# Loading the second half of the first tile by four transfers over 112, 16, 13 and 3 partitions

## The chip, the cores and the metric

The kernel runs on one core of one Trainium2 chip. The metric is the device time of one execution in microseconds (us); the time before is 469.24 us, the median of three executions (469.23 to 469.35). The profile and the trace are those of one further execution of 469.19 us, of which the profiler shows a span of 467.9 us.

In this kernel three of the core's engines do something: the scalar engine (ACT) computes the GELU, the vector engine (DVE) multiplies, and the sync engine (SP) does nothing but issue loads and the last stores. The bytes themselves are carried between HBM and SBUF by 16 DMA engines, which all transfers share. "DMA engine" always means one of these sixteen below.

## The reference

```python
def setup_inputs():
    batch, seq, dim = (32, 512, 2048)
    return {'x': np.random.randn(batch, seq, dim).astype(np.float32)}

def reference(x):
    half_dim = x.shape[-1] // 2
    x1, x2 = x[..., :half_dim], x[..., half_dim:]
    gelu_x1 = 0.5 * x1 * (1 + erf(x1 / np.sqrt(2)))
    return (gelu_x1 * x2).astype(np.float32)
```

Of each row of 2048 float32 numbers, the GELU of the first 1024 is multiplied by the other 1024. There are 16,384 rows: 134.2 MB are read and 67.1 MB written.

## The kernel before

The rows are taken in 16 tiles. A tile has 128 partitions with 8 rows in each, so that a partition's share of a load is one run of 64 KB in HBM and in SBUF, and of a store one run of 32 KB. Two input buffers and two output buffers are used in turn.

```python
R = 8
x_t = x_flat.rearrange("(n p r) d -> n p r d", p=P, r=R)      # P = 128, 16 tiles
o_t = out_flat.rearrange("(n p r) d -> n p r d", p=P, r=R)
x_bufs = [nc.alloc_sbuf_tensor(f"x{k}_tile", [P, R, dim], x.dtype) for k in range(2)]
o_bufs = [nc.alloc_sbuf_tensor(f"o{k}_tile", [P, R, half], out.dtype) for k in range(2)]
first = [nc.alloc_semaphore(f"first{j}") for j in range(2)]
ready = [nc.alloc_semaphore(f"ready{k}") for k in range(2)]
# ... more semaphores, and n[...], which counts what each was increased by ...

def load(i, rows, sem):
    ins = nc.sync.dma_start(out=x_bufs[i % 2][:, rows, :], in_=x_t[i][:, rows, :])   # L47
    counted(ins, sem, 16)
    return ins

def store(queue, i, rows, sem):
    queue.wait_ge(mul_done, n[mul_done.name])
    counted(queue.dma_start(out=o_t[i][:, rows, :],                                  # L54
                            in_=o_bufs[i % 2][:, rows, :]), sem, 16)

# the first tile in two halves, then the second tile whole
for ins in (
    load(0, slice(0, 4), first[0]),
    load(0, slice(4, 8), first[1]),
    load(1, slice(0, 8), ready[1]),
):
    ...

for i in range(n_tiles):
    k = i % 2
    last = i == n_tiles - 1
    pieces = i == 0 or last
    steps = ((0, 2), (2, 4), (4, 8)) if pieces else ((0, 5), (5, 8))
    for lo, hi in steps:
        rows = slice(lo, hi)
        if i == 0 and lo % 4 == 0:
            nc.scalar.wait_ge(first[lo // 4], 16)
        elif lo == 0:
            nc.scalar.wait_ge(ready[k], n[ready[k].name])
        # ACT:  o = gelu(x1)          (L81)
        # DVE:  o = o * x2            (L89), waits for the GELU
        if pieces and hi % 4 == 0:
            # store this half of the tile: from the scalar queue, the last tile's from SP
            ...
    if not pieces:
        # store the tile: from the scalar queue, that of the last but one from SP
        ...
    if i + 2 < n_tiles:
        nc.sync.wait_ge(mul_done, n[mul_done.name])
        load(i + 2, slice(0, R), ready[k])
```

The load of tile i + 2 is issued when tile i has been multiplied, as both use the same input buffer.

## Time and profile before

| what | before |
|---|---|
| time, median of 3 | 469.24 us (469.23 to 469.35) |
| span in the profile | 467.9 us |
| busy time of DVE | 140.5 us (30%) |
| busy time of ACT | 115.5 us (25%) |
| moved from and to HBM | 134.22 MB read, 67.11 MB written, 430 GB/s over the span |
| first half of the first tile landed, GELU begins | 12.76 us |
| second half landed, GELU begins | 22.46 us |
| second tile landed, GELU begins | 47.20 us |
| end of the last multiplication | 460.2 us |

How it is read: a share of the span beside an engine is its busy time. The landing times are the starts of the first GELU instructions after a wait for a load. The trace also holds a record of each DMA packet (start, duration, size, queue; not which of the sixteen engines carried it): a packet here is one partition's run, of 32 KB in the two loads of the first tile, 64 KB in the other loads, 32 KB in a store of a whole tile and 16 KB in a store of half a tile.

### The profile page before, as it was taken

Reading aid. Unit: us, or ns where it says so; the run is one execution under the profiler, and the core shown is the slowest. Engines: PE = TensorE matmul, PEld = TensorE weight load, DVE = VectorE, ACT = ScalarE, POOL = GpSimd, SP = SyncE. Lnnn points to the kernel's source line nnn. Section 1 sums busy time; section 2 is a strip of 40 time slices with the busy share of each in tenths; the row PEclk is TensorE's granted clock in tenths of the full one; section 3 lists DMA queues with packets and bytes.
Section 4 is the critical chain, followed back from the end, with each engine's and each line's share of the span. In section 5 each row is a group of like instructions: output and inputs, shape, how many; then the busy total and the mean of one; then the engine's idle time right before and its main releaser. Section 6 shows DMA issues by size and latency. Waiting matters only on the chain.

```text
span 467.9 us, 152 instructions
## 1 busy us (share of the span) xinstructions
DVE 140.5 (30%) x34; ACT 115.5 (25%) x35; POOL 0.2 (0%) x4
## 2 busy tenths in 40 slices
DVE  0330514207052060511606116060150702507043
ACT  1320606042060410604106050050500506014060
POOL 0000000000000000000000000000000000000000
DMA  8999999999999999999999999999999999999998
GB/s 359 448 448 443 403 405 492 409 403 448 459 437 403 434 417 493 403 403 448 476 420 403 445 406 493 403 406 445 487 409 403 445 451 448 403 434 417 493 389 373
DMA packets 5041, 201.34 MB, mean 430 GB/s; under 512 B 560, under 2 KB 560, under 8 KB 560
## 3 DMA queue, kind: packets, MB, share of 16 engines
q1 hardware_dynamic: 2880, 142.61, 70.6%
q10 hardware_dynamic: 2160, 58.72, 29.1%
q14 instruction: 1, 0.01, 0.0%
HBM read 134.22 MB, written 67.11 MB: 430 GB/s over the span
## 4 chain that ended last, share of the span: by engine, by line
DMA 76%; DVE 14%; ACT 8%; ACTq 0%; SPq 0%; issue 0%
DMA out_dram<-o_tile 66%; DVE o_tile L89 14%; DMA x_tile<-in_x_dram 10%; ACT o_tile L81 8%; ACTq L112 0%; SPq L47 0%
## 5 line engine op out<-in xcount | busy, mean ns | idle before, releaser
L89 DVE TENSOR_TENSOR o_tile<-o_tile,x_tile 128x5120 f32<-128x5120 f32 (+3 forms) x34 | 140.5, 4171 | 319.7 <-ACT o_tile L81 319.7
L81 ACT ACTIVATE o_tile<-x_tile 128x5120 f32<-128x5120 f32 (+3 forms) x34 | 114.3, 3407 | 337.4 <-DMA out_dram<-o_tile 301.6
L81 ACT ACT_TABLE_LOAD x1 | 1.3, 1283 | 2.9 <-PEq L67 2.9
L135 POOL MEMSET const-bfloat16-1.0<- 128x1 bf16 x1 | 0.1, 101 | 0.0
L135 POOL MEMSET const-uint8-127<- 128x1 uint8 x1 | 0.1, 101 | 0.0
L135 POOL MEMSET const-float32-0.0<- 128x1 f32 x1 | 0.1, 98 | 0.2 <-issue 0.2
L135 POOL MEMSET const-float32-1.0<- 128x1 f32 x1 | 0.1, 98 | 0.0
## 6 DMA issues: line engine op xcount, KB each, us to landing
out_dram<-o_tile ACTq DMA_DIRECT2D x13, 4096.0 KB, 44.7
x_tile<-in_x_dram SPq DMA_DIRECT2D x2, 4096.0 KB, 16.6
out_dram<-o_tile ACTq DMA_DIRECT2D x2, 2048.0 KB, 34.5
out_dram<-o_tile SPq DMA_DIRECT2D x1, 4096.0 KB, 25.2
out_dram<-o_tile SPq DMA_DIRECT2D x2, 2048.0 KB, 7.8
x_tile<-in_x_dram SPq DMA_DIRECT2D x15, 44.2
```

Of the source, the lines that this page charges most:

```text
L81: nc.scalar.activation(out=o_bufs[k][:, rows, :], in_=x_bufs[k][:, rows, :half], func=GELU),
L89: nc.vector.tensor_mul(out=o_bufs[k][:, rows, :], in0=o_bufs[k][:, rows, :], in1=x_bufs[k][:, rows, half:],),
L135: nc = _bacc.Bacc("TRN2", target_bir_lowering=False, num_devices=1)
```

## The change

The load of rows 4 to 7 of the first tile, which was one transfer over 128 partitions, becomes four transfers on the same queue: rows 4 to 7 of partitions 0 to 111; rows 4 to 6 of partitions 112 to 127; row 7 of partitions 112 to 124; row 7 of partitions 125 to 127. One row is 8 KB. If the first two are shared by all 16 DMA engines, the third by 13 and the fourth by 3, thirteen of the sixteen carry at least as much as before and three carry less: the engines' shares, 256 KB each before, become 264 KB for three, 256 KB for ten and 248 KB for three. It is meant to even out small differences between the moments at which the DMA engines finish. The wait for the second half is raised from 16 to the sum of the four transfers' increments, 64; nothing else differs.

```diff
-    def load(i, rows, sem):
-        ins = nc.sync.dma_start(out=x_bufs[i % 2][:, rows, :], in_=x_t[i][:, rows, :])
+    def load(i, rows, sem, parts=slice(0, P)):
+        ins = nc.sync.dma_start(out=x_bufs[i % 2][parts, rows, :], in_=x_t[i][parts, rows, :])
         counted(ins, sem, 16)
         return ins
 ...
         load(0, slice(0, 4), first[0]),
-        load(0, slice(4, 8), first[1]),
+        load(0, slice(4, 8), first[1], slice(0, 112)),
+        load(0, slice(4, 7), first[1], slice(112, 128)),
+        load(0, slice(7, 8), first[1], slice(112, 125)),
+        load(0, slice(7, 8), first[1], slice(125, 128)),
         load(1, slice(0, 8), ready[1]),
 ...
             if i == 0 and lo % 4 == 0:
-                nc.scalar.wait_ge(first[lo // 4], 16)
+                nc.scalar.wait_ge(first[lo // 4], n[first[lo // 4].name])
```

## The prediction

> **What bounds the kernel now.** I read the head of the page first: engines, the forty slices, DMA.

> ```profile
> span 467.9 us, 152 instructions
> DVE 140.5 (30%) x34; ACT 115.5 (25%) x35; POOL 0.2 (0%) x4
> ...
> DMA  8999999999999999999999999999999999999998
> ...
> q1 hardware_dynamic: 2880, 142.61, 70.6%
> q10 hardware_dynamic: 2160, 58.72, 29.1%
> q14 instruction: 1, 0.01, 0.0%
> HBM read 134.22 MB, written 67.11 MB: 430 GB/s over the span
> ```

> The compute engines are busy 30% and 25%. The DMA row has nines except in its end slices, and the two data queues together take 70.6 + 29.1 = 99.7% of all sixteen DMA engines' time. There is next to nothing left to fill: the bound is bytes per DMA engine.

> The chain that ended last says the same, step after step of it being a transfer; its beginning is what the change touches:

> ```profile
> 1.64 45.54 DMA x_tile<-in_x_dram
> 47.18 0.02 issue
> 47.20 4.48 ACT o_tile L81
> 51.68 0.02 issue
> 51.70 8.77 DVE o_tile L89 x2
> 60.48 0.02 issue
> 60.50 40.04 DMA out_dram<-o_tile
> ```

> The ACT and DVE links in it are no time without transfers. I asked for the busy time by stage, cut where the first half, second half and second tile land and where the last tile's GELU begins (columns: stretch, its length, DVE, ACT and POOL busy with counts, clock, DMA share, GB/s):

> ```profile
> 0.00:12.74 12.74, 0.00 (x0) 1.28 (x1) 0.20 (x4) 1.00 0.91 370
> 12.74:22.44 9.70, 4.49 (x2) 3.71 (x2) 0.00 (x0) 1.00 1.15 486
> 22.44:47.18 24.74, 4.42 (x1) 3.62 (x1) 0.00 (x0) 1.00 0.98 424
> 47.18:448.54 401.36, 122.65 (x28) 99.72 (x28) 0.00 (x0) 1.00 1.00 432
> ```

> In the 401 us of the middle the DMA share is 1.00 at 432 GB/s while DVE works 123 us. (The 1.15 is packets booked to one side of a cut.) Last I took the packet records themselves. They don't name the DMA engine, but each packet starts within some nanoseconds of another's end, so they can be strung into sixteen chains. The sixteen first packets start at 1.74 to 2.30 us, the sixteen last end at 466.92 to 467.43 us, and no chain has a gap of more than 3 ns. Each chain carries 12.58 MB; a 32 KB packet takes 1.21 us (27 GB/s), one of 64 KB 2.42 us. Of the sixteen ends, two are late: 467.40 (the chain with the one 8 KB instruction packet of 0.31 us, at 460.9 us) and 467.43 (the chain that started last, at 2.30 us). Then come 467.26 and 467.23, the others being at 467.15 or before.

> So whatever one DMA engine loses, anywhere, it finishes later by the same amount, and the slowest of sixteen sets the end. There is no slack to take it up, except that an engine which isn't last has up to 467.43 - 466.92 = 0.5 us.

> [...]

> **The change part by part.**

> *Shares.* 224 + 24 + 8 + 8 = 264 KB for the first three engines, 256 KB for ten, 224 + 24 = 248 KB for the last three. 8 KB is a quarter of a packet of 1.21 us, 0.30 us. If nothing else changed, the best is the case that the latest finishers get less: 467.43 would become 467.13, and the next one, 467.40, has to be among the relieved too. Then 467.26 stands (if it isn't), a gain of 0.17 us. The worst is that the chain at 467.40 is one of the three that get more: 467.70, a loss of 0.27 us. As the first three start first (1.74 to 1.75 us, if starts go by number) and the chain with the instruction packet started at 1.744 us, I lean to the loss. Either way 0.06% at most.

> *Issue.* Three more issues on SP at about 0.43 us (the longest of the loads' issue times in the trace) delay the second tile's load by 1.3 us. It was issued by 1.64 us and isn't needed until the second half has been carried, about 20 us. Nothing on the path.

> *Waits.* The wait for 64 instead of 16 adds none by itself. If the second half lands late by a few us, GELU, multiplication, the store of that half (30.57 us) and the load of the third tile shift likewise; the DMA engines still have the second tile's 8 packets of 2.42 us, 19.3 us, to carry, against 22.46 to 30.57 = 8.1 us of compute and issue, so none runs dry.

> *Ports.* This is the part that matters, [...] The 112-partition transfer: 7 packets per engine. If each takes 7 partitions in a row (that is my assumption; [...]), engines start at partitions 0, 7, 14, ... 105; [...] Engines 0 to 2 then lose 2.42 + 2.72 + 0.91 + 0.61 + 0.30 (their own 8 KB) = 6.96 us; less the up to 0.5 us by which they were early, the end moves by 6.5 to 7.0 us: 475.7 to 476.2 us.

> **The rivals.** First, [...] only the shares count, 469.07 to 469.51 us. For it: the change aims at tenths of a us, and someone who tunes on that scale will have seen how the DMA engines finish. [...] I give it 25%.

> Second, the limit holds but costs half: [...] 3 to 5 us, 472 to 474 us. Nothing in the trace speaks for or against. With the full count, 60%.

> Third, the 112 partitions are dealt one by one, engine after engine. Then at each step the sixteen engines write sixteen neighbouring partitions, [...] so up to 498 us and slower by 6%. [...] 15%.

> **Range and chances.** The middle of this mixture lies in the port case, somewhat below its full count: 474.0 us. The range takes in the first rival at its low end and the full count with some 2 us to spare: 468.9 to 478.4. The 2% lines are 459.9 and 478.6 us; faster is out of reach, since the whole idle time at the ends is about 5 us; above 478.6 lies the third rival nearly alone: 0.12.

> **What would show it.** With the ports right, the packet records of the changed kernel have packets of 24 KB at up to 3.6 us and of 8 KB at around 1.2 us instead of 0.9 and 0.3, and 32 KB packets at 1.21 and 2.42 us mixed; the second half lands at 26 to 30 us instead of 22.46; the second tile lands 4 to 7 us later than 47.18; and the sixteen chains end apart by some us instead of 0.5. With the first rival, 24 KB take 0.91 us, the landing moves by under 0.5 us and the ends stay within 0.8 us. I am wrong altogether if 24 KB packets run alone at full speed and the time still moves by more than 0.3 us, or if they are slow and the end doesn't move: then the engines had slack that I don't see.

## The result and the profile after

The changed kernel takes 477.1 us (median of five runs, 476.86 to 477.24) against 469.28 us for the kernel before in the same session (469.23 to 469.35): a ratio of 1.0165, 95% interval 1.0151 to 1.0179. That is 7.8 us slower. The prediction had 474.0 us with a range of 468.9 to 478.4, and 475.7 to 476.2 for the full sum of its port case.

The head of the page of the changed kernel, to be laid beside the lines shown of before:

```profile
span 475.9 us, 155 instructions
DVE 140.5 (30%) x34; ACT 115.5 (24%) x35; POOL 0.2 (0%) x4
...
DMA  8999999999999999999999999999999999999998
GB/s 353 286 332 430 437 443 408 427 452 441 421 438 443 408 432 457 438 410 449 446 405 435 454 441 410 454 435 424 421 443 421 441 454 430 427 419 443 441 410 362
...
q1 hardware_dynamic: 2928, 142.61, 70.8%
q10 hardware_dynamic: 2160, 58.72, 28.8%
HBM read 134.22 MB, written 67.11 MB: 423 GB/s over the span
```

Compute is the same to a tenth of a us, the bytes are the same, and the DMA engines are as busy as before: the row of nines has not changed. What has changed are two slices of the GB/s row, which in the kernel before reads:

```profile
GB/s 359 448 448 443 403 405 492 409 403 448 459 437 403 434 417 493 403 403 448 476 420 403 445 406 493 403 406 445 487 409 403 445 451 448 403 434 417 493 389 373
```

In the second and third slice (11.9 to 35.7 us) the same busy DMA engines move 286 and 332 GB/s; before it was 448 and 448. From the fourth slice on nothing is unusual. This is a loss that a busy share cannot show: a packet that takes longer (1.969 us for 32 KB where it was 1.213, as the packet records below show) keeps its engine busy longer.

The stages, cut where the halves and the second tile land and where the last tile's GELU begins (columns as in the prediction):

```profile
0.00:12.97 12.97, 0.00 (x0) 1.28 (x1) 0.20 (x4) 1.00 0.93 364
12.97:35.21 22.24, 4.49 (x2) 3.71 (x2) 0.00 (x0) 1.00 0.99 287
35.21:57.33 22.12, 4.42 (x1) 3.62 (x1) 0.00 (x0) 1.00 1.02 441
57.33:456.00 398.67, 122.64 (x28) 99.72 (x28) 0.00 (x0) 1.00 1.00 433
456.00:475.88 19.88, 8.92 (x3) 7.22 (x3) 0.00 (x0) 1.00 0.91 389
```

The last stage of the kernel before, for comparison:

```profile
448.54:467.90 19.36, 8.92 (x3) 7.21 (x3) 0.00 (x0) 1.00 0.95 407
```

From the first half's landing to the second's it is 22.24 us instead of 9.70, 12.5 us more. The next two stages give back 2.6 and 2.7 us, because in the long second stage the engines also carried store packets which the kernel before carries in its later stages: by the end of the last packet of the first tile's load, 91 store packets of 16 KB are done (at 34.02 us), in the kernel before none (at 22.07 us). With +0.2 us at the start and +0.5 at the end the sum is the 8.0 us between the spans. The chain's beginning shows the same wait:

```profile
2.58 32.62 DMA x_tile<-in_x_dram
35.21 0.02 issue
35.23 3.62 ACT o_tile L86
```

The packet records say which packets grew (mean duration; the 32 KB packets are those of the 112-partition transfer):

| packets | alone, in the kernel before | changed kernel | more per DMA engine |
|---|---|---|---|
| 7 of 32 KB per engine | 1.213 us | 1.969 us (1.49 to 2.38) | 7 x 0.756 = 5.29 us |
| 1 of 24 KB per engine | 0.91 us (three quarters of 1.213) | 2.317 us (1.60 to 2.60) | 1.41 us |
| 16 of 8 KB in all | 0.30 us (a quarter) | 0.309 us (0.309 to 0.313) | 0.0 us |
| stores of 16 KB, those before 60 us | 0.611 us | 0.672 us, 209 packets (up to 1.286) | 209 x 0.061 / 16 = 0.80 us |

Together 7.5 us per engine on average; the sixteen engines' last packets end 7.6 us later on average. The last data packet of the last engine ends at 475.49 us instead of 467.42, 8.07 us later, and the engines' ends now lie 1.27 us apart instead of 0.51.

### The profile page after: what moved, and what is told of

It is laid out like the page before. It is cut to its first block, busy times and chain, and to the rows that moved or that the text cites. A ratio compares the mean times of both kernels' runs of the same rounds, so it can differ in the third digit from the quotient of the medians.

```text
span 475.9 us, 155 instructions
## 1 busy us (share of the span) xinstructions
DVE 140.5 (30%) x34; ACT 115.5 (24%) x35; POOL 0.2 (0%) x4
## 2 busy tenths in 40 slices
DMA  8999999999999999999999999999999999999998
## 3 DMA queue, kind: packets, MB, share of 16 engines
q1 hardware_dynamic: 2928, 142.61, 70.8%
q10 hardware_dynamic: 2160, 58.72, 28.8%
HBM read 134.22 MB, written 67.11 MB: 423 GB/s over the span
## 4 chain that ended last, share of the span: by engine, by line
DMA 71%; DVE 15%; ACT 8%; another core or an unknown queue 3%; ACTq 0%; SPq 0%; issue 0%
DMA out_dram<-o_tile 64%; DVE o_tile L94 15%; ACT o_tile L86 8%; DMA x_tile<-in_x_dram 7%; ACTq L117 0%; SPq L47 0%; ACTq L54 0%
## 5 line engine op out<-in xcount | busy, mean ns | idle before, releaser
L94 DVE TENSOR_TENSOR o_tile<-o_tile,x_tile 128x5120 f32<-128x5120 f32 (+3 forms) x34 | 140.5, 4171 | 327.7 <-ACT o_tile L86 327.7
```

Source lines behind the costliest of these rows:

```text
L94: nc.vector.tensor_mul(out=o_bufs[k][:, rows, :], in0=o_bufs[k][:, rows, :], in1=x_bufs[k][:, rows, half:],),
```

## The experiments

The theory, in the recorded texts, has the name **ports**: DMA engines that write certain partitions at the same time hold each other up, and the sets of 112 and 16 partitions cause that. What holds them up was the author's estimate and no trace shows it; what the runs show is how long the packets of a set take. The rivals are **shares** (the uneven 8 KB), **count** (more transfers on the queue), and **HBM** (the engines read rows at other distances from each other). All experiments alter the loads of the first tile's second half only.

| kernel | time, us | ratio to before, 95% interval | mean 32 KB packet |
|---|---|---|---|
| 112 + 16, even shares | 477.35 | 1.0174 (1.0157 to 1.0191) | 1.960 us |
| row 7 alone over 112, 13, 3 | 471.58 | 1.0046 (1.0031 to 1.0061) | none in the half |
| four of 128 partitions | 469.38 | 0.9997 (0.9989 to 1.0006) | none in the half |
| 128 partitions at another HBM pitch | 469.33 | 1.0003 (0.9995 to 1.0012) | 1.213 us |
| 64 + 64 | 478.46 | 1.0197 (1.0181 to 1.0212) | 2.36 us |
| 8 x 16 neighbours | 493.65 | 1.0518 (1.0503 to 1.0534) | 3.96 us |
| 8 x 16, every eighth | 478.19 | 1.0190 (1.0173 to 1.0207) | 2.30 us |
| 8 x 16 neighbours, read as every eighth | 493.65 | 1.0519 (1.0497 to 1.0542) | 3.96 us |
| 7 x 16, every seventh, + 16 | 477.76 | 1.0182 (1.0166 to 1.0197) | 2.02 us (the seven) |
| 4 x 16, every fourth from 32, + 32 + 32 | 473.85 | 1.0092 (1.0075 to 1.0110) | 1.213, then 2.43 us |
| 13 partitions of 8 KB more | 469.72 | 1.0007 (0.9999 to 1.0015) | 1.213 us |
| 4 x 16, every fourth from 28, + 16 + 12 + 32 + 4 | 486.38 | one run | see there |

**Even shares.**

```diff
         load(0, slice(4, 8), first[1], slice(0, 112)),
-        load(0, slice(4, 7), first[1], slice(112, 128)),
-        load(0, slice(7, 8), first[1], slice(112, 125)),
-        load(0, slice(7, 8), first[1], slice(125, 128)),
+        load(0, slice(4, 8), first[1], slice(112, 128)),
```

> Second half of the first tile in two transfers, 112 and 16 partitions with four rows each: every DMA engine carries 256 KB again. Ports theory [...]: the 112-partition packets stay slow (2.0 us mean for 32 KB instead of 1.21, +5.3 us per engine), the 16-partition ones too (about +1.9 us), so 476 to 477.2 us. Shares theory (the uneven 8 KB make the loss): back to 469.3 us. Count theory (each extra transfer costs): one extra instead of three, a third of the loss, 471.9 us. HBM theory [...]: the 112-partition part stays, 474.6 us or more.

477.35 us: the loss is all there without uneven shares and with half the transfers. The 112-partition packets take 1.960 us, those of the 16 partitions 3.585 us for 32 KB (+2.4 us). Shares and count fall as causes, and the split into 16, 13 and 3 costs nothing that shows: if anything the changed kernel is 0.25 us faster than this one.

**The same shares with a quarter of the bytes in question.**

```diff
-        load(0, slice(4, 8), first[1], slice(0, 112)),
-        load(0, slice(4, 7), first[1], slice(112, 128)),
+        load(0, slice(4, 7), first[1]),
+        load(0, slice(7, 8), first[1], slice(0, 112)),
         load(0, slice(7, 8), first[1], slice(112, 125)),
         load(0, slice(7, 8), first[1], slice(125, 128)),
```

> Rows 4 to 6 over all 128 partitions, and row 7 alone over 112, 13 and 3: the same number of transfers and the same uneven shares (264, 256, 248 KB) as the changed kernel, but only a quarter of the bytes in the 112-partition transfer and no 16-partition transfer. Ports theory: a quarter of 5.3 us = 1.3 us, and 0 to 1 us for 13 and 3: 470.6 to 471.6 us. Shares theory and count theory: 477.1 us as the changed kernel.

471.58 us, at the edge of what the ports theory expected and 5.5 us below what the other two did. The 24 KB packets of the 128-partition transfer take 0.912 us all, the 8 KB ones 0.470 us on average instead of 0.30.

**The count alone.** Four transfers of 128 partitions, one row each (`load(0, slice(r, r + 1), first[1])` for r = 4 to 7 in place of the four).

> Second half in four transfers of one row each, all over 128 partitions: the number of transfers of the changed kernel without its partition sets. Ports, shares and HBM theories: 469.3 us, packets of 8 KB at 0.30 us. Count theory: 477.1 us.

469.38 us against 469.32 before, and the 8 KB packets at 0.309 us (0.321 at most). Three more transfers on the queue cost nothing.

**The HBM side alone.** The half's 128 partitions are filled at once, from rows 14p + 4 to 14p + 7 in place of 8p + 4 to 8p + 7; that half's values are those of other rows.

```diff
+    wide = x_flat[0 : 128 * 14, :].rearrange("(n p r) d -> n p r d", p=P, r=14)
...
+        load_from(wide[0][0:128, 4:8, :], slice(4, 8), first[1], slice(0, 128)),
```

> Second half in one transfer over 128 partitions, but read from HBM at a pitch of 14 rows (112 KB) per partition instead of 8 (64 KB), [...]. (The values of that half are other rows' values then.) HBM theory: the 32 KB packets of that half take about 2 us and the time is about 474.6 us. Ports theory: 1.21 us a packet and 469.3 us.

469.33 us and 1.213 us a packet. Reading at 112 KB from partition to partition instead of 64 KB costs nothing. That this sets the engines as far apart as the changed kernel does was the author's estimate; the crosswise kernel below tests the HBM side in another way.

**Half the partitions at a time.** `slice(0, 64)` and `slice(64, 128)`, four rows each.

> Second half in two transfers over partitions 0 to 63 and 64 to 127, four partitions per DMA engine in each. Ports theory with four partitions in a row per engine: [...] every 32 KB packet takes twice 1.21 = 2.42 us, +9.7 us in eight packets: 479.0 us. Ports theory with partitions dealt one by one: [...] 4.84 us a packet, +29 us: 498 us. [...]

478.46 us. In the second to fourth step of sixteen packets the mean is 2.55 to 2.56 us, with all sixteen alike. The time fits the 479.0 us expected with four partitions in a row per engine. A dealing one by one is ruled out: it would have the engines write sixteen neighbours at each step, and those take 4.45 us in the next kernel.

**Sixteen neighbours, and every eighth.** Eight transfers over 16 partitions each, first neighbours (`slice(16 * j, 16 * j + 16)`), then every eighth (`slice(j, 128, 8)`).

> Second half in eight transfers of 16 neighbouring partitions, one partition per engine, [...]. Ports theory: 4.84 us per 32 KB packet, +29 us, 498 us [...]. Count theory has fallen already (four transfers of 128 partitions cost nothing); [...].

> Second half in eight transfers of 16 partitions each, every eighth partition (j, j+8, ..., j+120): the same count and sizes as eight transfers of 16 neighbours, [...]. Ports theory: 2.42 us per packet, +9.7 us, 479 us. If 16-partition transfers are slow for another reason than ports: about what the neighbours take, 498 us.

493.65 and 478.19 us. Same sizes, same number of transfers, same rows read; only which partitions go together differs, and it is worth 15.5 us. The GB/s rows of the two pages (first the neighbours), for the second and third slices:

```profile
GB/s 367 117 154 193 424 420 452 420 436 436 442 431 426 436 420 458 428 428 442 415 452 412 450 420 428 455 420 447 410 439 442 434 447 431 418 442 434 447 407 365
```

```profile
GB/s 352 220 352 410 448 429 440 432 426 423 467 404 448 429 440 423 440 451 404 448 429 440 415 448 451 412 440 462 407 426 448 440 412 440 467 388 443 445 412 380
```

117 and 220 GB/s in the second slice, against 448 before: a quarter and a half. The steady steps take 4.45 us per 32 KB packet for the neighbours and 2.55 for every eighth. The neighbours come out 4.4 us below the 498 expected: the steady 4.45 us is less than the 4.84 expected, and in the last three transfers, where store packets come between, the packets take 3.3 to 3.5 us.

**Which side, crosswise.** The slow SBUF side of the one with the HBM side of the other (that half's rows land in other partitions):

```diff
+    load_from(x_t[0][j:128:8, 4:8, :], slice(4, 8), first[1], slice(16 * j, 16 * j + 16))   # j = 0 to 7
```

> As the eight transfers of 16 neighbouring partitions, but each is read from every eighth partition's rows in HBM (512 KB apart instead of 64 KB), so that the SBUF side is that of the slow version (493.65 us) and the HBM side that of the strided version (478.2 us). (That half's rows land in other partitions then.) Ports theory: 493.6 us, 4.45 us a packet. HBM theory: 478.2 us, 2.55 us a packet.

493.65 us, the same to the hundredth as with neighbours on both sides. The partitions written decide, not the rows read. The fourth corner (every eighth partition filled from neighbouring rows) was not run.

**How 112 partitions are dealt.** Seven transfers `slice(j, 112, 7)`, j = 0 to 6, then 112 to 127.

> Partitions 0 to 111 in seven transfers of 16 partitions each, every seventh one (j, j+7, ..., j+105), then 112 to 127 as one: each engine gets partitions 7e to 7e+6 one after the other, which is what I assumed for the dealing of the 112-partition transfer. If that dealing is right: the same time as the 112 and 16 split, 477.3 us, and 32 KB packets of about 1.96 us mean in the seven steps. If the 112 partitions are dealt otherwise: a clearly different mean; [...].

477.76 us, 2.02 us per packet. Taken in groups of sixteen in order of start, the mean packets follow each other in the same pattern as in the two kernels with a 112-partition transfer:

```
step                          1     2     3     4     5     6     7
changed kernel, us         1.78  2.25  2.17  1.80  1.71  1.99  2.07
112 + 16                   1.86  2.20  2.17  1.76  1.65  2.02  2.06
seven of every seventh     1.98  2.16  2.23  1.88  1.70  1.99  2.19
```

So the assumption of seven partitions in a row per engine fits: with it made explicit, the means differ by 0.12 us at most from those of the changed kernel in all steps but the first (0.20). After the first step, the fourth and fifth are the fastest in all three. And all packets are slower than 1.21 us, not only those of some engines: in the second step of the changed kernel all sixteen take 2.24 to 2.31 us.

**Sixteen partitions at full rate.** Partitions 32+j, 36+j, ..., 92+j in one transfer, for j = 0 to 3; the rest in two of 32.

```diff
+        load(0, slice(4, 8), first[1], slice(32 + j, 93 + j, 4)),    # j = 0 to 3
+        load(0, slice(4, 8), first[1], slice(0, 32)),
+        load(0, slice(4, 8), first[1], slice(96, 128)),
```

> Partitions 32 to 95 in four transfers of 16 partitions, every fourth one (32+j, 36+j, ... 92+j), [...]; then 0 to 31 and 96 to 127 in a transfer each (two packets per engine, [...]). Ports theory: the first four 32 KB packets of each engine take 1.21 us as in the 128-partition transfer, though the transfers have 16 partitions; the last four 2.42 to 2.55 us, so +4.9 to 5.3 us, 474.1 to 474.5 us. If 16-partition transfers are slow in themselves: 2 us and more in the first four too, 478 us or more.

473.85 us, just under the 474.1 to 474.5 expected. All 64 packets of the first four transfers take 1.213 us, shortest and longest; the first 32-partition transfer then starts at 16.8 us with 2.25 and 2.55 us. With this set, packets of a transfer of 16 partitions are as fast as those of one of 128 (1.213 us both). The second slice of its page stands at 311 GB/s, between the 448 of before and the 220 of every eighth partition:

```profile
GB/s 355 311 399 444 444 433 411 411 433 488 399 416 438 477 399 444 416 472 399 430 458 444 399 438 449 408 435 444 455 433 402 441 477 411 405 438 488 399 416 383
```

**What the aim itself was worth.** The kernel before with one load more, of row 7 into 13 partitions of the second output buffer, where it is overwritten before use; the second tile's GELU waits for it.

```diff
+        nc.sync.dma_start(out=o_bufs[1][32:81:4, 0:2, :], in_=x_t[0][32:81:4, 7, :] ...)   # increases "extra" by 16
...
+                if i == 1:
+                    nc.scalar.wait_ge(extra, 16)
```

> The kernel before with one more load of 8 KB to each of 13 partitions (32, 36, ... 80, [...]), [...] to a place that is overwritten later; 13 to 15 carry as much as before. It asks what the aim of the change, relieving engines 13 to 15 by 8 KB, is worth [...]. If the two DMA engines that end last (467.40 and 467.43 us) are both among 13 to 15, the end moves by at most 0.14 us (467.26 + 0.30 against 467.43), and relieving them could have gained up to 0.17 us. If one of them is among 0 to 12, the end moves by 0.27 to 0.30 us, and nothing was to be gained.

469.72 us (14 runs) against 469.31: 0.41 us by the medians, though the interval of the ratio reaches from -0.05 to +0.7 us. That speaks for the second case, and somewhat beyond its 0.30. (The numbers 0 to 12 stand for the thirteen engines of the extra load; that they are the thirteen which the change does not relieve was assumed and is not shown.) The packet chains cannot settle which engine it is. The chain with the instruction packet of 8 KB has 12.599 MB, 8 KB more than it had before, and ends at 467.86 us (the last chain of all at 468.12), which would put its DMA engine among 0 to 12. But wherever two packets start within a nanosecond or two of each other the chains can be swapped, and followed back from the instruction packet at 461 us, this chain could be any of more than half of the sixteen at 22 us.

**Do held-up engines slow the others?** The 112-partition packets lost 5.3 us where the prediction's sum had 2.42. The sets are those of the full-rate kernel, begun at 28 instead of 32. Two outcomes were named: 8 of the 64 packets are slow, or most of them are.

```diff
+        load(0, slice(4, 8), first[1], slice(28 + j, 89 + j, 4)),    # j = 0 to 3
+        # then partitions 0-15, 16-27, 92-123 and 124-127
```

> Why the 112-partition packets lost 5.3 us per engine and not the 2.4 us [...]. Four transfers of 16 partitions 28+j, 32+j, ... 88+j [...], then the remaining partitions in four smaller ones. If [...]: in the first four steps 8 of the 64 packets of 32 KB take about 2.55 us and the other 56 take 1.21 us. If [...]: most of the 64 take clearly more than 1.21 us, [...]. The total isn't of interest [...], about 477 to 482 us.

Two of the sixteen engines, the pair, are slower than the rest. In the first step the pair takes 1.68 and 1.99 us, and the other fourteen engines 1.36 to 1.40, against 1.213 with the sets from 32: all are held up a little. In the second step the pair takes 2.45 and 2.48 us and the others 1.22 to 1.25, and in the third and fourth step too the unpaired stay at 1.21 to 1.25 us, but for one of 1.37 at the end. So here a lone pair slows hardly anyone but itself once it has begun (1.21 to 1.25 us for the others); in the step in which it begins, all sixteen are slower. In these steps the "most of the 64" case has fallen.

What follows is not so simple. The third packets of the pair itself take 3.27 and 3.84 us and the fourth 4.2 us each. From 17.2 us on the other fourteen have gone on to partitions 0 to 15 and beyond; that their writing there slows the pair is likely by the time at which it happens, but no run separates it. The total of 486.38 us holds the four transfers of the rest, and is not compared.

## Why the prediction was right, and where its sum was not

The time lay in the range, and the loss is the one that the prediction put first, in the transfers over 112 and 16 partitions: the sum of its port case was 6.5 to 7.0 us and 7.8 us came. The 474.0 us were lower because they mixed in two rivals.

*Shares.* Bounded at 0.06% in the prediction; the kernel with even shares is as slow as the changed one. Right. The lean to a loss is not shown: the start of 1.744 us for the chain with the instruction packet was no safe reading, as chains cross on the way, and no run tells whether its engine is one of the three that get more. What relieving three engines could have brought can be bounded: if at least one of the two latest ends is not theirs, for which the 0.41 us of the extra load speak under the assumption named there, it is no more than 467.43 - 467.40 = 0.03 us of that profile.

*Issue and waits.* Right: four transfers of 128 partitions cost nothing, and the DMA row keeps its nines in the stages after. (Eight packets of 2.42 us are 19.4 us, not 19.3, and the idle time at the ends is about 4 us, not 5; nothing hangs on either.) The landings fit 16, 16, 13 and 3 engines for the four transfers: the second half's semaphore is increased 50 times, twice before any of its data (at 2.7 and 3.0 us) and 48 times with it, 16 + 16 + 13 + 3.

*The sum, term by term.*

| term | predicted for engines 0 to 2 | measured |
|---|---|---|
| 112 partitions | +2.42 us | +5.29 us (mean of all engines) |
| 16 partitions, 24 KB | +2.72 us | +1.41 us |
| 13 and 3 partitions | +0.91 and +0.61 us | 0.0 us |
| own 8 KB | +0.30 us | not told apart |
| stores held up | not seen | +0.80 us |

So the sum came out near because errors of both signs met, which is luck. Its terms were the author's estimate, and nothing in the trace of before tests them, as all its transfers span 128 partitions. The term that failed is that of the 112 partitions, which counted two packets of seven as twice as long: twice is about right for the pair in the second step of the one-pair kernel (2.45 and 2.48 us against 1.213) and for every eighth partition (2.55), but here nearly every packet was slow (1.49 to 2.38 us). What I can show is the pattern by steps, that the other fourteen engines were slower by 0.15 to 0.19 us in the step in which the pair began, and that the pair went from 2.5 to 4.2 us after the others had gone on to other partitions. Whether such beginnings and such slowing make up the rest of the 5.29 us is not shown. It stays open.

The 16-, 13- and 3-partition terms were too high. The engines no longer started together: the 24 KB packets start over 1.0 us and the 8 KB packets over 3.5 us (30.2 to 33.7). That they hold each other up less for this reason is likely, but no run separates it. And nothing in the prediction had the store packets slow down, though the same DMA engines carry them between the loads (91 by 34.02 us): the slow ones, up to 1.29 us instead of 0.61, all start between 25.3 and 34.0 us, while the first tile's load is still under way.

*What would show it.* Of the signs that were named, the slow 24 KB packets came at 1.6 to 2.6 us and not 3.6, the 8 KB packets at 0.31 and not 1.2, the 32 KB packets spread from 1.49 to 2.38 us instead of a mixture of 1.21 and 2.42, and the ends 1.27 us apart. The second half's landing, put at 26 to 30 us, was at 35.2, and the second tile landed 10.2 us later, not 4 to 7: both were worked out from the losses of the sum alone, without the 91 store packets that the engines carry while the load takes longer. Those are no loss, as the later stages show.

*Rivals.* The first, shares alone, would have had packets of 24 KB at 0.91 us, and they took 2.317; fallen. "Costs half" had the sum wrong (3 to 5 us, and 7.8 came). "Dealt one by one" would be the 16 neighbours again and again, at 4.45 us; the 64 + 64 kernel (2.55 to 2.56 us) and the 112 partitions themselves (1.969 us) rule it out.

## What to carry to other kernels

## What the runs showed that I had not expected

Every eighth partition takes 2.55 us per 32 KB, 2.1 times 1.213; sixteen neighbours take 4.45 us, 3.7 times, where I had expected 2.42 and 4.84. Worked out from these packet times, sixteen engines move 16 x 32.8 KB / 2.55 us = 206 GB/s and 16 x 32.8 KB / 4.45 us = 118 GB/s, by the side of 220 and 117 in the second slices of their pages.

Store packets belong to transfers over all 128 partitions, and still took up to 1.29 us instead of 0.61 while the slow loads were under way on the same DMA engines (0.866 us on average for the 128 of them up to 52.2 us in the kernel of eight times 16 neighbours).
